# A gated delta-net kernel: state scaling, value masks and small copies made on GpSimd

## The chip, the cores and the metric

The kernel runs on one core of a Trainium2 chip. The time is the device time of one execution in microseconds; a run's figure is the median of its executions, and the chip's profiler records one execution more, with every instruction of every engine. The engines are named as the profile names them: PE (TensorE matmul), PEld (its weight loads), DVE (VectorE), ACT (ScalarE), POOL (GpSimd) and SP (which issues the DMAs). Each engine runs its own queue strictly in order, and engines wait for each other on semaphores.

## The reference, cut to what matters

A two-layer decoder step: an mLSTM layer, then a gated delta-net layer, each followed by an MLP and LayerNorms. 512 prompt tokens and 8 sequences of 4 sample tokens go through together, 544 columns in all. In the delta-net layer the projected rows pass a causal convolution of width 4; the chunked form inverts a triangular matrix for each chunk and head; and every head's state S is decayed and updated.

```python
xp = jnp.concatenate([conv0, qkv], axis=1)            # 3 rows of history, then the new rows
c = xp[:, 0:T] * conv_w[0]
for j in range(1, CONV_W):
    c = c + xp[:, j:j + T] * conv_w[j]
c = jax.nn.silu(c)
new_conv = xp[:, T:]
...
A = M + jnp.eye(L)                                    # M strictly lower triangular
sol = lax.linalg.triangular_solve(A, rhs, left_side=True, lower=True)
...
S = gL_c[..., None, None] * S + jnp.einsum('bhsk,bhsv->bhkv', kdec_c, v_new)
```

## The kernel before

All matrices are held transposed, with features on the 128 partitions and the 544 columns along the free side. A projection (`proj`, L193, through `mm3`, L153) splits each 128x1024 weight tile into two fp32r halves on ACT (L111) and DVE (L112) and issues 48 matmuls of 272 columns on line L158. These are the bulk of PE's work and fill the time between the steps of the delta-net layer.

That layer has eight units of two heads. The list `ORDER` (L58) names its steps, letter and unit: `p` projects and convolves, `a` prepares (`prepare`, with a long chain of small DVE instructions on `xb`, L1085 and L1087, and a DMA round trip that lands as the tile `xc`), `i` inverts (`invert`), `s` scans, `d` decodes the sample tokens of two units, `u` updates their states, `y` and `w` gate and project the output. The steps of `a i s d u` are recorded at a higher priority, and a list scheduler of the language interleaves everything; what comes out is one fixed order for each engine. In what follows i0 to i7 are the eight inversions and u0 to u3 the four updates.

The parts that the change touches:

- `conv`: zeroes three columns of the tile `pre` (L947), copies the old rows into it (L948), lets ACT fill in the new ones, copies 27 columns out through `cvo` (L953, L954), and multiplies by the weights (L958 on ACT, L960 on DVE). Lines L967 and L972 then form the sample part of the result in two instructions.
- `project`: copies one 32-column block of `kqx` to its neighbour (L998).
- `invert`: spreads `xc` over the block-diagonal tile `X` with one masked product of 1024 columns (L1102); PE transposes `X` next (L1117).
- `decode`: for each sample sequence copies 32 columns into one of two buffers `kz` (L1241), the weights of eight small matmuls (L1244).
- `update`: for each half `q` of the eight sequences it makes two value masks `VM` of 512 columns (L1328), in two buffers that both halves share, so the masks of the second half must wait for the matmuls of the first. For each head pair `h0` it loads two state tiles `sst` (`state`, four buffers shared with `decode`), issues six matmuls (L1337) into two PSUM banks, and for each of four sequences of a tile takes state times decay plus product (L1344), then stores the tile (L1345).

The PSUM tag `s`, which those two banks belong to, has two buffers in all (`BANKS`, L37), and `scan` and `decode` use them too.

## Time and profile before

| | |
|---|---|
| median of 3 runs | 1838.17 us (1834.11 to 1847.94) |
| the profiled execution's own time | 1844.15 us |
| its span, first to last instruction | 1842.4 us |
| mean granted PE clock over the span | 0.98 of full speed |
| instructions on POOL | 40, 18.6 us busy |

Sums that come out of the profile are made against 1844.15 us. The delta-net layer lies between about 690 and 1480 us of the span. A granted clock of 1.00 is PE's upper level of 2.4 GHz, and 0.50 its lower one of 1.2 GHz. PE's instructions are pipelined, and the end of a matmul is modelled, so a high busy share of PE does not by itself say that nothing waits.

### The profile page before, as it was taken

The numbers are of one execution on the slowest core, as the hardware profiler recorded it, in microseconds if no ns is written. First come the engines' busy times: TensorE is split into PE (matmuls) and PEld (weight loads), VectorE is DVE, ScalarE is ACT, GpSimd is POOL, SyncE is SP. The second block draws the span as 40 slices with busy tenths as digits, with TensorE's granted clock in tenths as the row PEclk, the third lists the DMA queues.
The fourth block names the chain that finished last, engine by engine and source line by source line (L and its number), as shares of the span: only waits on it lengthen the run. The fifth ranks groups of instructions, "written<-read, shape, count | busy, mean of one in ns | idle before, by whom it ended". The sixth has DMA issues, their size and how long they took to land.

```text
span 1842.4 us, 34187 instructions
## 1 busy us (share of the span) xinstructions
PE 1784.1 (97%) x13868; PEld 1697.9 (92%) x13868; DVE 1070.9 (58%) x2638; ACT 834.8 (45%) x1894; POOL 18.6 (1%) x40
## 2 busy tenths in 40 slices
PE   7999999999999999899999999999999999999997
PEld 7999998999999998897988898899888999999996
DVE  7464767432344377775767757775768643234436
ACT  6454356421233157673657356446436532124314
POOL 2000000000000000000000000000000000000000
PEclk9999999999999998997999999999999999999998
DMA  4122222232233221313232423331332222322311
GB/s 159 58 104 70 70 86 92 81 92 85 88 92 104 85 63 58 102 44 120 58 99 63 127 65 103 100 101 59 88 107 84 81 92 81 92 91 82 113 60 50
DMA packets 84286, 158.78 MB, mean 86 GB/s; under 512 B 37536, under 2 KB 41504, under 8 KB 83616
## 3 DMA queue, kind: packets, MB, share of 16 engines
q1 hardware_dynamic: 84128, 156.60, 28.0%
q8 instruction: 109, 1.79, 0.4%
q14 instruction: 49, 0.40, 0.1%
HBM read 140.51 MB, written 16.06 MB: 85 GB/s over the span
## 4 chain that ended last, share of the span: by engine, by line
PE 82%; DVE 9%; ACT 5%; DMA 3%; issue 1%; SPq 0%; ACTq 0%; DVEq 0%
PE pg_t L158 39%; PE pm_s L158 12%; PE pm_a L158 12%; PE pm_a L1111 4%; PE pm_s L1337 1%; PE pm_s L1181 1%; DVE lnt L342 1%; DVE lnt L343 1%; PE pm_s L1193 1%; PE pm_a L1051 1%; PE pm_s L1201 1%; PE pm_s L1244 1%; DVE acc L960 1%; PE pm_a L1132 1%; PE pm_s L1211 1%
## 5 line engine op out<-in xcount | busy, mean ns | idle before, releaser
L112 DVE TENSOR_TENSOR wl<-wraw,wh 128x1024 fp32r<-128x1024 f32 x200 | 244.7, 1223 | 371.4 <-ACT wh L111 367.6
L158 PE MATMUL pg_t<-XH,wh 128*128 128x272 f32 x1480 | 440.2, 298 | 8.8 <-ACT XH L111 7.2
L158 PE MATMUL pg_t<-XH,wl 128*128 128x272 f32 x1480 | 435.1, 294 | 0.5 <-DVE wl L112 0.5
L158 PE MATMUL pg_t<-XL,wh 128*128 128x272 f32 x1480 | 434.9, 294 | 0.0
L111 ACT CAST wh<-wraw 128x1024 fp32r<-128x1024 f32 (+1 forms) x201 | 210.4, 1047 | 480.7 <-PE pg_t L158 234.6
L158 PEld LDWEIGHTS pg_t<-XH,wh 128*128 128x128 f32 x1480 | 280.6, 190 | 12.5 <-ACT XH L111 7.2
L158 PEld LDWEIGHTS pg_t<-XH,wl 128*128 128x128 f32 x1480 | 280.0, 189 | 2.7 <-issue 1.3
L158 PEld LDWEIGHTS pg_t<-XL,wh 128*128 128x128 f32 x1480 | 280.4, 189 | 2.0 <-issue 1.0
L158 PE MATMUL pg_t<-h,wh 128*128 128x272 f32 x672 | 129.1, 289 | 0.0
L158 PEld LDWEIGHTS pg_t<-h,wh 128*128 128x128 f32 x672 | 105.7, 188 | 0.3
L158 PE MATMUL pg_t<-h,wl 128*128 128x272 f32 x336 | 96.9, 288 | 0.0
L158 PE MATMUL pm_a<-h,wh 128*128 128x272 f32 x496 | 95.3, 288 | 0.0
L158 PE MATMUL pm_s<-h,wh 128*128 128x272 f32 x496 | 94.9, 288 | 0.0
L158 PE MATMUL pm_s<-XH,wh 128*128 128x272 f32 x288 | 84.4, 293 | 0.0
L158 PE MATMUL pm_s<-XH,wl 128*128 128x272 f32 x288 | 83.9, 291 | 0.0
L158 PE MATMUL pm_s<-XL,wh 128*128 128x272 f32 x288 | 83.7, 291 | 0.0
L158 PE MATMUL pm_a<-XL,wh 128*128 128x272 f32 x280 | 81.6, 291 | 1.0 <-DVE XL L354 0.8
L158 PE MATMUL pm_a<-XH,wh 128*128 128x272 f32 x280 | 82.0, 293 | 0.1
L158 PE MATMUL pm_a<-XH,wl 128*128 128x272 f32 x280 | 80.7, 288 | 0.0
L960 DVE SCALAR_TENSOR_TENSOR acc<-pre,cst,acc 128x568 f32<-128x568 f32 x96 | 76.8, 800 | 4.7 <-ACT acc L958 4.3
L158 PEld LDWEIGHTS pm_s<-h,wh 128*128 128x128 f32 x496 | 77.9, 188 | 0.2
L158 PEld LDWEIGHTS pm_a<-h,wh 128*128 128x128 f32 x496 | 78.0, 188 | 0.1
(558 smaller groups left out, 3938.0 us busy)
## 6 DMA issues: line engine op xcount, KB each, us to landing
wraw<-in_w SPq DMA_DIRECT2D x64, 512.0 KB, 3.6
wraw<-in_wb SPq DMA_DIRECT2D x48, 512.0 KB, 3.6
wraw<-in_w2a SPq DMA_DIRECT2D x32, 512.0 KB, 3.6
wraw<-in_wa SPq DMA_DIRECT2D x24, 512.0 KB, 3.6
wraw<-in_w2b SPq DMA_DIRECT2D x24, 512.0 KB, 3.7
sst<-in_s0b SPq DMA_DIRECT2D x32, 256.0 KB, 3.4
sst<-in_s SPq DMA_DIRECT2D x32, 256.0 KB, 3.4
out_ss<-sst SPq DMA_DIRECT2D x32, 256.0 KB, 2.3
```

Of the source, the lines that this page charges most:

```text
L111: S.copy(hi, src)
L112: V.tensor_tensor(lo, src, r32(hi), op=ALU.subtract)
L158: T.matmul(ps, lhsT=wt[:, k, :], rhs=xt[k][:, HS[h]], start=first and k == 0 and q == 0, stop=last and k == n - 1 and q == 2,)
L342: V.tensor_tensor(t, x, rs, op=ALU.mult)
L343: V.tensor_tensor(t, t, mu, op=ALU.subtract)
L960: V.scalar_tensor_tensor(acc, pre[:, q:q + WC], cw[q], acc, op0=ALU.mult, op1=ALU.add)
L1051: T.matmul(pk[:, q * 256:(q + 1) * 256], lhsT=kq[:, 0, c0:c0 + P], rhs=kq[:, :, c0:c0 + P], start=True, stop=True)
L1111: T.matmul(ps[:, c], lhsT=left[:, c], rhs=right[:, c], start=True, stop=True)
L1132: T.transpose(pt[:, c], X[:, c0 + c, 0:m], ident)
L1181: T.matmul(pks[:, w], lhsT=kq[:, w, cc], rhs=St, start=True, stop=True)
L1193: T.matmul(pv[:, j], lhsT=X[:, 4 * (ch // 2) + 2 * j + ch % 2], rhs=rhs[:, j] if ch else vtok[:, j, 0], start=True, stop=True)
L1201: T.matmul(pS, lhsT=ktok[:, ch], rhs=vd, start=True, stop=True)
```

## The change

Six groups of instructions go from DVE to POOL: the zeroing and the copies of `conv`, the copy of `kqx`, the product that makes `X` (one instruction becomes eight, one for each 16-column block), the copies into `kz`, and the masks `VM` (one of 512 columns becomes four of 128). In `update` the state tile is now multiplied by its decay on POOL ahead of time, four instructions of 128 columns for a tile, and what stays on DVE is one addition of 512 columns. The sample part of the convolution's result becomes one instruction in place of two, for which the tile `acc` is three columns wider.

```diff
--- before.py
+++ after.py
@@ -944,16 +944,17 @@
 
 
             pre = cv("pre", W)
-            V.memset(pre[:, 0:3], 0.0)
-            V.tensor_copy(samp(pre)[:, :, 0:3], cvt[:, slot])
+            G.memset(pre[:, 0:3], 0.0)
+            G.tensor_copy(samp(pre)[:, :, 0:3], cvt[:, slot])
             S.copy(pre[:, 3:3 + HN], pss[0])
             S.copy(pre[:, 3 + HN:3 + TP], pss[1][:, :TP - HN])
             S.copy(samp(pre)[:, :, 3:7], pss[1][:, TP - HN:HN].rearrange("p (b t) -> p b t", t=TS))
             cvo = gp.tile([P, 27], F32, tag="cvo", name="cvo", bufs=2)
-            V.tensor_copy(cvo[:, 0:3], pre[:, TP:TP + 3])
-            V.tensor_copy(cvo[:, 3:27].rearrange("p (b t) -> p b t", t=3), samp(pre)[:, :, 4:7])
+            G.tensor_copy(cvo[:, 0:3], pre[:, TP:TP + 3])
+            G.tensor_copy(cvo[:, 3:27].rearrange("p (b t) -> p b t", t=3), samp(pre)[:, :, 4:7])
             dma(o_conv[:, ct, :], cvo)
-            acc = cv("acc", WC)
+            accw = cv("acc", W)
+            acc = accw[:, 0:WC]
             cw = [cst[:, C_CW + 4 * ct + q:C_CW + 4 * ct + q + 1] for q in range(4)]
             S.activation(acc, pre[:, 0:WC], AF.Copy, scale=cw[0])
             for q in range(1, 4):
@@ -963,13 +964,8 @@
             dp = acc[:, 0:TP] if dp is None else dp
             V.tensor_tensor(dp, acc[:, 0:TP], sgm[:, 0:TP], op=ALU.mult)
 
-            a3, s3 = acc[:, TP + 3:WC], sgm[:, TP + 3:WC]
-            V.tensor_tensor(
-                ds[:, 0:7],
-                a3[:, 0:49].rearrange("p (b t) -> p b t", t=7)[:, :, 0:4],
-                s3[:, 0:49].rearrange("p (b t) -> p b t", t=7)[:, :, 0:4],
-                op=ALU.mult)
-            V.tensor_tensor(ds[:, 7], a3[:, 49:53], s3[:, 49:53], op=ALU.mult)
+            a3, s3 = (t[:, TP + 3:W].rearrange("p (b t) -> p b t", t=7)[:, :, 0:4] for t in (accw, pre))
+            V.tensor_tensor(ds, a3, s3, op=ALU.mult)
             return dp, pre[:, 0:TP]
 
         def spare():
@@ -995,7 +991,7 @@
                 pss = first.pop(0) if first else proj(wb[base + w])
                 xs = kqx[:, w, j0].rearrange("p (b t) -> p b t", t=TS)
                 dst, sq = conv(ct + w, cvt, w, kq[:, w], xs, pss)
-                V.tensor_copy(kqx[:, w, j0 + 1], kqx[:, w, j0])
+                G.tensor_copy(kqx[:, w, j0 + 1], kqx[:, w, j0])
                 pt = mtile("t")
                 if w == 0:
                     for ch in range(NCH):
@@ -1099,9 +1095,8 @@
 
             U = st["U"]
             X = tl("X", n=8, bufs=NX)
-            V.tensor_tensor(
-                X.rearrange("p s (b j) -> p s b j", j=16), st["xc"].unsqueeze(2).to_broadcast([P, 8, 8, 16]),
-                bm16.unsqueeze(1).unsqueeze(3).to_broadcast([P, 8, 8, 16]), op=ALU.mult)
+            for b in range(8):
+                G.tensor_scalar(X[:, :, 16 * b:16 * b + 16], st["xc"], bm16[:, b:b + 1], None, op0=ALU.mult)
             def half(t, w, o):
                 return t.rearrange("p c (b x) -> p c b x", x=2 * w)[:, :, :, o:o + w]
 
@@ -1238,7 +1233,7 @@
                 kz.append(z.rearrange("p (r h x) -> p r h x", r=2, h=4))
             for bb in range(NB):
                 st, z = state(s0b[g, :, bb]), kz[bb % 2]
-                V.tensor_copy(z[:, :, :, 28:32], ua["kqx"][:, :, :, TS * bb:TS * bb + TS])
+                G.tensor_copy(z[:, :, :, 28:32], ua["kqx"][:, :, :, TS * bb:TS * bb + TS])
                 for w in range(2):
                     for h in range(4):
                         T.matmul(pkq[32 * h:32 * h + 32, w], lhsT=z[:, w, h, 28 - TS * bb:60 - TS * bb], rhs=st[:, h],
@@ -1325,11 +1320,16 @@
                 VM = []
                 for w in range(2):
                     VM.append(tl("VM", ("tok", "sx")[w], dt=F32R))
-                    V.tensor_tensor(VM[w], vhl[:, w:w + 1].to_broadcast([P, 4, P]),
-                                    bmask[:, 4 * q:4 * q + 4].unsqueeze(2).to_broadcast([P, 4, P]), op=ALU.mult)
+                    for r in range(4):
+                        G.tensor_scalar(VM[w][:, r], vhl[:, w], bmask[:, 4 * q + r:4 * q + r + 1], None, op0=ALU.mult)
                 for h0 in (0, 2):
 
+                    glc = (ua if h0 == 0 else ub)["glc"]
                     sts = [state(s0[g, :, h, 4 * q:4 * q + 4]) for h in (h0, h0 + 1)]
+                    for j in range(2):
+                        for r in range(4):
+                            bb = NCH + 4 * q + r
+                            G.tensor_scalar(sts[j][:, r], sts[j][:, r], glc[:, j, bb:bb + 1], None, op0=ALU.mult)
                     pS = [mtile("s").rearrange("p (b d) -> p b d", b=4) for _ in range(2)]
                     for i, (a, b) in enumerate(((0, 0), (0, 1), (1, 0))):
                         for j in range(2):
@@ -1337,11 +1337,7 @@
                             T.matmul(pS[j], lhsT=khr[o:o + 32, a], rhs=VM[b][o:o + 32], start=(i == 0), stop=(i == 2),
                                      tile_position=(o, 0))
                     for j in range(2):
-                        glc = (ua if h0 == 0 else ub)["glc"][:, j]
-                        for r in range(4):
-                            bb = 4 * q + r
-                            t = sts[j][:, r]
-                            V.scalar_tensor_tensor(t, t, glc[:, NCH + bb:NCH + bb + 1], pS[j][:, r], op0=ALU.mult, op1=ALU.add)
+                        V.tensor_tensor(sts[j], sts[j], pS[j], op=ALU.add)
                         dma(o_ss[g, :, h0 + j, 4 * q:4 * q + 4], sts[j])
 
         def gate_out(g, oTs, osm):
```

The scheduler lays out a new order from this. Three places of it matter for the prediction. The first is PE in u1, between the last matmuls (L1337) on the masks of the first half and the first ones on those of the second, before; the rows left out are 27, of them 21 projections (L158):

```order
L1337 MATMUL pm_s<-VM,khl 128x512 x3
L158 MATMUL pg_t<-gyh,wh 128x272
...
L158 MATMUL pg_t<-gyl,wh 128x272
L158 MATMUL pg_t<-gyh,wl 128x272
L1337 MATMUL pm_s<-VM,khl 128x512 x6
L1027 MATMUL pm_t<-ident,acc 128x128 x4
L1337 MATMUL pm_s<-VM,khl 128x512 x6
```

The same place after, line L1337 as before:

```order
L1056 MATMUL pm_a<-RRb,hmr 128x256 x2
L1337 MATMUL pm_s<-VM,khl 128x512 x3
L158 MATMUL pg_t<-gyh,wh 128x272
L158 MATMUL pg_t<-gyl,wh 128x272
L158 MATMUL pg_t<-gyh,wl 128x272
L158 MATMUL pg_t<-gyh,wh 128x272
L158 MATMUL pg_t<-gyl,wh 128x272
L158 MATMUL pg_t<-gyh,wl 128x272
L1337 MATMUL pm_s<-VM,khl 128x512 x6
L158 MATMUL pg_t<-gyh,wh 128x272
```

Between the two halves there stood 30 rows of PE's queue; now there are six projections.

The second place is the making of those masks for the second half of u1. Before, it stands on DVE, where U and A are products of `prepare`:

```order
L1344 SCALAR_TENSOR_TENSOR sst<-sst,glc,pm_s 128x128
L1069 TENSOR_TENSOR A<-pm_a,Eh 128x256
L1344 SCALAR_TENSOR_TENSOR sst<-sst,glc,pm_s 128x128
L1328 TENSOR_TENSOR VM<-vhl,bmask 128x512 x2
L1068 TENSOR_TENSOR U<-pm_a,Eh 128x256
L1069 TENSOR_TENSOR A<-pm_a,Eh 128x256
```

After, it stands on POOL, where X is the inversion's tile (L1099), VM the masks (L1324) and sst the scaled states (L1332):

```order
L947 MEMSET pre 128x3
L948 COPY pre<-cvt 128x8x3
L1099 TENSOR_SCALAR X<-xc,bm_150 128x8x16 x8
L953 COPY cvo<-pre 128x3
L954 COPY cvo<-pre 128x24
L1324 TENSOR_SCALAR VM<-vhl,bmask 128x128 x8
L1332 TENSOR_SCALAR sst<-sst,glc 128x128 x16
L1232 MEMSET kz 128x480 x2
L1099 TENSOR_SCALAR X<-xc,bm_150 128x8x16 x8
```

Two instructions of DVE have become eight of POOL, behind copies of the convolution and ahead of 16 state scalings.

The third is PE around the first transposes of `X` in i0, where `sx` belongs to the decode step; before:

```order
L1282 MATMUL pm_s<-ident,sx 128x128
L158 MATMUL pg_t<-XH_75,wh 128x272
L158 MATMUL pg_t<-XL_83,wh 128x272
L158 MATMUL pg_t<-XH_75,wl 128x272
L158 MATMUL pg_t<-XH_76,wh 128x272
L158 MATMUL pg_t<-XL_84,wh 128x272
L158 MATMUL pg_t<-XH_76,wl 128x272
L158 MATMUL pg_t<-XH_77,wh 128x272
L158 MATMUL pg_t<-XL_85,wh 128x272
L1117 MATMUL pm_a<-ident,X 128x128 x8
L1287 MATMUL pm_s<-sx 128x128
```

And after, with the transposes on L1112:

```order
L1277 MATMUL pm_s<-ident,sx 128x128
L158 MATMUL pg_t<-XL_90,wh 128x272
L158 MATMUL pg_t<-XH_82,wl 128x272
L158 MATMUL pg_t<-XH_75,wh 128x272
L158 MATMUL pg_t<-XL_83,wh 128x272
L158 MATMUL pg_t<-XH_75,wl 128x272
L158 MATMUL pg_t<-XH_76,wh 128x272
L158 MATMUL pg_t<-XL_84,wh 128x272
L158 MATMUL pg_t<-XH_76,wl 128x272
L1112 MATMUL pm_a<-ident,X 128x128 x8
L1282 MATMUL pm_s<-sx 128x128
```

The transposes still stand behind eight projections; the work ahead of them that makes `X` has moved to POOL.

## Rows read from the trace of the kernel before

**Rows 1.** The page's head and part 1: busy time of each engine.

```profile
span 1842.4 us, 34187 instructions
...
PE 1784.1 (97%) x13868; PEld 1697.9 (92%) x13868; DVE 1070.9 (58%) x2638; ACT 834.8 (45%) x1894; POOL 18.6 (1%) x40
```

**Rows 2.** The page's part 4: the chain that ended last, by engine.

```profile
PE 82%; DVE 9%; ACT 5%; DMA 3%; issue 1%; SPq 0%; ACTq 0%; DVEq 0%
```

**Rows 3.** Busy time by stretch: PE, PEld, DVE, ACT, POOL, granted PE clock, DMA share.

```profile
400.00:500.00 100.00, 100.00 (x800) 100.00 (x799) 28.22 (x34) 20.30 (x23) 0.00 (x0) 1.00 0.29 89
690.00:1480.00 790.00, 764.61 (x5941) 698.27 (x5939) 562.35 (x1638) 443.46 (x1129) 4.71 (x9) 0.96 0.30 86
754.30:757.80 3.50, 0.29 (x3) 0.07 (x1) 3.50 (x11) 2.56 (x4) 0.00 (x0) 0.99 0.01 2
757.80:761.20 3.40, 3.10 (x14) 2.94 (x14) 3.40 (x19) 3.37 (x12) 0.00 (x0) 0.50 0.11 18
832.40:839.60 7.20, 4.35 (x25) 2.92 (x23) 6.67 (x21) 1.05 (x1) 0.00 (x0) 1.00 0.61 166
839.60:863.50 23.90, 23.90 (x108) 19.27 (x107) 10.60 (x31) 7.73 (x18) 0.93 (x2) 0.50 0.42 132
```

**Rows 4.** PE's waits, 690 to 1480 us: total us, times, longest us.

```profile
PE pm_t L1002 <- DVE xb L1087: 3.5, 1, 3.5
PE pm_s L1337 <- DVE VM L1328: 2.3, 1, 2.3
...
PE pm_s L1337 <- DVE sst L1344: 1.4, 2, 0.8
```

**Rows 5.** Groups of POOL's instructions, by shape: busy us, mean ns, idle before.

```profile
L280 POOL TENSOR_SCALAR_AFFINE_SELECT bd<-bd 128x128 f32<-128x128 f32 x2 | 2.2, 1104 | 0.0
...
L279 POOL TENSOR_SCALAR_AFFINE_SELECT bd<-o 128x128 f32<-128x128 f32 x2 | 1.2, 622 | 0.0
...
L244 POOL TENSOR_SCALAR_AFFINE_SELECT b<-b 128x128 f32<-128x128 f32 x1 | 0.5, 538 | 0.0
L243 POOL TENSOR_SCALAR_AFFINE_SELECT b<-z 128x128 f32<-128x128 f32 x1 | 0.5, 517 | 0.0
...
L237 POOL TENSOR_SCALAR_AFFINE_SELECT f<-z 128x128 f32<-128x128 f32 x1 | 0.3, 292 | 0.0
L252 POOL TENSOR_SCALAR_AFFINE_SELECT rowm<-o 128x32 f32<-128x32 f32 x1 | 0.2, 217 | 0.0
```

**Rows 6.** Groups of DVE's instructions, by shape, columns as above.

```profile
L1344 DVE SCALAR_TENSOR_TENSOR sst<-sst,glc,pm_s 128x128 f32<-128x128 f32 x128 | 36.3, 342 | 21.9 <-PE pm_s L1337 21.0 <-DMA sst<-in_s 0.6
...
L964 DVE TENSOR_TENSOR acc<-acc,pre 128x512 f32<-128x512 f32 x16 | 10.9, 683 | 2.2 <-ACT pre L475 2.0
...
L1328 DVE TENSOR_TENSOR VM<-vhl,bmask 128x512 fp32r<-128x512 f32 x16 | 10.5, 682 | 0.0
...
L1102 DVE TENSOR_TENSOR X<-xc,bm 128x1024 f32<-128x1024 f32 x8 | 9.7, 1218 | 0.3 <-DMA xc<-dx 0.3
...
L948 DVE COPY pre<-cvt 128x24 f32<-128x24 f32 x32 | 5.8, 183 | 0.0
...
L947 DVE MEMSET pre<- 128x3 f32 x32 | 2.0, 61 | 0.1
```

**Rows 7.** Timelines of DVE and PE at i0, i4 and i6: start us, duration us.

```profile
774.62 1.23 DVE L1102 TENSOR_TENSOR X<-xc,bm 128x1024 f32<-128x1024 f32 x1 [0.28 <-DMA xc<-dx]
...
775.90 1.09 PE L1117 MATMUL pm_a<-ident,X 128*128 128x128 f32 x8
...
1048.49 1.22 DVE L1102 TENSOR_TENSOR X<-xc,bm 128x1024 f32<-128x1024 f32 x1
...
1058.51 1.04 PE L1117 MATMUL pm_a<-ident,X 128*128 128x128 f32 x8
...
1234.90 1.22 DVE L1102 TENSOR_TENSOR X<-xc,bm 128x1024 f32<-128x1024 f32 x1
...
1240.77 0.71 PE L1117 MATMUL pm_a<-ident,X 128*128 128x128 f32 x5
```

## The prediction

> **What bounds the kernel now.** I read the page's head first: PE is busy 97% of the span, DVE 58%, POOL 1% [rows 1]; then the chain that ended last, 82% of it PE [rows 2]. So time taken off DVE counts only where PE stands waiting for DVE, and time added to POOL counts only where PE ends up waiting for POOL. Next the stretches [rows 3]. In 400:500 PE issues 800 projections in 100 us, 0.125 us each, which is as dense as it gets and my price for one projection as cover. In 690:1480, the delta-net layer, PE is idle for 790 - 764.6 = 25.4 us, and the granted clock averages 0.96, so some 0.04 x 790 = 32 us of clock are lost. These two, 57 us, are all that the layer can give back, whatever DVE is spared.
>
> How the clock is lost shows in the same group: PE is busy for 0.29 of 3.5 us (754.3:757.8) and the next 3.4 us run at 0.50, the 1.2 GHz level; it is busy for 4.35 of 7.2 us (832.4:839.6, inside u0) and the next 23.9 us run at 0.50, filled with the small matmuls of i1 and u0. An idle gap of 2.3 to 3.5 us [rows 4] is thus paid a second time: 3.4 us at half speed lose at least 1.7 us, and the long stretch up to 12.
>
> **What one POOL instruction costs.** The trace of before has no multiplication on POOL. Its nearest rows are nine affine selects of 128x128 f32, which read SBUF and write SBUF: two of 1104 ns, two of 622, one of 538, one of 517, one of 292 and two more rows that repeat it [rows 5]; mean 0.60 us. A mask, a state scaling and a block of X each cover 128 columns too. I take 0.60 and keep 0.29 and 1.10 as ends. The small copies (24 to 32 columns) I take at the 0.2 us of the 32-column select [rows 5], against 0.18 on DVE [rows 6]. In total: 256 instructions x 0.60 + 144 copies x 0.2 = 182 us of POOL over some 600 us, so POOL does not become a bound by its sum; it counts where a burst of eight stands in front of PE.
>
> The Trainium skill (GPSIMD Engine Reference, section 4.1, Engine selection) calls one-input work on GpSimd roughly line-rate, which would put these instructions at the lower end, 0.29 us, and the time near that of rival (c) below. The selects are one-input work as well, and six of the nine took 517 ns or more, so the rows speak for more than that.
>
> **Part 1: the masks.** Eight instructions of 0.60 us, 4.8 us, replace two of DVE of 0.68. The second half's masks share their buffers with the first's, so POOL can begin only when the last matmul of the first half has read them, and PE cannot go on before the last is written. What stands between the two on PE is therefore the whole cover, in the new order ten projections in u0 (1.25 us), six in u1 (0.75), six in u3 (0.75), and in u2 six small matmuls and a transpose, 0.13 us each by the eight transposes in 1.04 us [rows 7], so 0.9. PE waits 4 x 4.8 - 3.65 = 15.6 us; 2.3 of that is there already [rows 4]. **+13 us** (at 0.29: +3; at 1.10: +29). In u1 the cover shrank from 30 rows of the queue to six.
>
> **Part 2: X.** Eight instructions, 4.8 us, replace one of 1.2 [rows 6]: +3.6 us between the landing of `xc` and the transposes. In i0 the transposes start 0.05 us after X is done [rows 7]; this stands for five of the eight inversions (0.05 to 0.33 us). i5 has 1.1 us to spare, i4 8.8 and i6 4.6 [rows 7]. Five at 3.5 and one at 2.5 make 20. Two places move: i1's transposes now stand behind 44 more projections (5.5 us), which covers it, -3.5; i6's lose 47 projections (5.9 us) and with them their spare time, +4. **+20 us** (at 0.29: +5; at 1.10: +45).
>
> **Part 3: scaled states.** PE never reads them; it waits only through the two banks of tag `s`, which the addition on DVE must empty. Both pairs of the first half are scaled long before. In the second half a pair of tiles is scaled by 4.8 us after the masks and added by 5.5. Against PE's order this fits in u1 and u2, and is late by about 1 us in u0, where the X of i1 stands between the two tiles, and by 0.8 in u3. **+2 us** (0 to +17). What queues behind a late addition: on DVE the weight splits L112, on SP the store L1341 and behind it the next weight load.
>
> **Part 4: small work.** The copies into `kz` have two buffers and come one by one between matmuls, as before: +1 (0 to +5). In the convolution the zeroing and the copy of old rows now stand behind bursts of 16 to 32 POOL instructions, 10 to 19 us; ACT's L958 waits for them, and behind it on ACT the emptying of the projection banks. Mostly a tile is prepared well ahead, so with SP's share from part 3 I take +4 (0 to +10). The copies to `cvo` are hidden: only a store waits for them. The wider `acc` and the merged product cost nothing that PE sees.
>
> **Part 5: the clock.** Six new gaps of 2.5 to 4 us (X; the updates u1 to u3 have their half-speed stretches already) at 1.7 us: **+10** (0 to +17). Against it, the new order puts projections among the matmuls of i1 and u0, and the 23.9 us at half speed should mostly go: **-8** (0 to -12).
>
> **Part 6: DVE's relief.** State: 36.3 - 32 x 0.68 = 14.4 us; masks 10.5; X 9.7 [rows 6]; six small groups, from the 5.8 of L948 down to the 2.0 of L947 [rows 6], 26 together; the merged pair 5. That is 66 us off DVE's 562 in this layer [rows 3]. PE sees of it what it waited for DVE here: the 1.4 us for the state updates [rows 4] and a part of the 3.5 us for `xb` and the shorter waits like it: **-6** (0 to -12).
>
> **The sum.** 13 + 20 + 2 + 1 + 4 + 10 - 8 - 6 = +36 us. Against the profiled execution's 1844.15 that is 1880; that execution lies 6 us above the median of the runs, so I predict **1874 us**, 2% slower.
>
> **The rivals.** (a) POOL and DVE get in each other's way. DVE is busy 71% of the layer [rows 3], mostly with instructions of 0.2 to 1.2 us [rows 6]; if a POOL instruction often has to let one of these finish, 0.25 us on top of 0.60 is a fair mean. At 0.85 us the masks cost +21, X +32, states and queues +13, the clock +10, the gains shrink to -9: +67, **1905 us**. In the trace of before POOL is idle beside DVE, apart from the setup, so nothing speaks for or against it. The Trainium skill states this rule (SBUF — State Buffer, Who interferes with whom): a DVE instruction with two SBUF inputs contends with a GpSimd instruction that reads SBUF, and the later one waits for the whole of the other. No row here shows it. It speaks against this change, since the additions, the splits L112 and the convolution L960 are of that kind.
>
> (b) PE's gaps are mostly waits that would have come anyway. While PE stands for POOL, DVE and ACT catch up, and half of the 25 idle us of before vanish (-13), and the clock does not fall for the X gaps (-10): +13, **1851 us**. For it: the idle time is in many short waits. Against: the gaps of before each stand at one line for one producer [rows 4].
>
> (c) Faster. The place is u0 with i1: the half-speed stretch after 839.6 goes entirely (-12), the relief is whole (-12), and POOL's price is at the lower end, so that masks and X cost only +3 and +5, the rest +2: -14, **1824 us**. It turns on one number, POOL's instruction: at 0.35 us masks and X cost about 12 and the sum crosses zero; below that the kernel is faster. One of the groups in [rows 5] is below it, three of its nine instructions.
>
> **How the numbers follow.** Forecast 0.42, (a) 0.17, (b) 0.25, (c) 0.16. A measurement of this kernel can tell about 1%, 18 us, from no change. Slower by more than that are the forecast and (a): 0.59. (c) is split, since 1824 is within 1%: faster by over 1% 0.11, and within 1% 0.30. The range leaves out the far half of (a), and half of (c): 1822 to 1912. With the price at its upper end everywhere the sum would be far above, about +120; I leave that out, since only two of the nine selects were that long.
>
> **What would show it.** In the profile after, POOL's groups for VM, X and sst at 0.5 to 0.7 us each (below 0.35: (c); above 0.8: (a)); PE waiting for POOL at the matmuls of `update` for 3 to 5 us in each of four places, and at the transposes of X for 2.5 to 4 us in five or six; no wait of PE for VM on DVE; the granted clock above 0.9 where u0 and i1 lie, but short half-speed stretches behind the gaps at X; DVE at about 1005 us busy (more means that it is held up by POOL). The forecast is wrong if PE's waits for POOL add up to under 15 us, or if the stretches at half speed shrink by more than the gaps add.

## The result, and the profile after

The changed kernel takes 1926.69 us (median of 4 runs, 1923.26 to 1929.63) against 1841.22 for the kernel before: ratio 1.0464, 95% interval 1.0417 to 1.0511. It is 85.5 us slower where 36 were forecast, and above the upper end of the range, 1912.

The page of the changed kernel, head, part 1 and part 4 [rows 1, 2]:

```profile
span 1927.9 us, 34433 instructions
...
PE 1816.9 (94%) x13868; PEld 1722.6 (89%) x13868; DVE 1033.6 (54%) x2310; ACT 832.3 (43%) x1894; POOL 244.6 (13%) x472
...
PE 28%; DVE 4%; POOL 2%; DMA 2%; ACT 1%; issue 1%; SPq 0%; POOLq 0%; ACTq 0%; DVEq 0%
```

DVE is busy 37 us less, POOL 226 us more, and PE, which runs the same 13868 instructions, is busy 33 us *more*. Most of that is the clock's, as the next rows show. They give the layer and its half-speed stretches by window (columns as in [rows 3]): first the layer of the kernel before, two of its seven stretches and the sum of all seven; then the layer of the changed kernel, five of its 17 stretches and the sum of all 17:

```profile
690.00:1479.90 789.90, 764.51 (x5940) 698.17 (x5939) 562.25 (x1638) 443.39 (x1128) 4.71 (x9) 0.96 0.30 86
...
1181.01:1187.83 6.82, 6.82 (x32) 4.42 (x31) 4.32 (x14) 2.02 (x4) 0.00 (x0) 0.50 0.56 174
...
1355.09:1361.91 6.82, 6.82 (x25) 5.46 (x27) 4.50 (x13) 0.00 (x0) 0.00 (x0) 0.50 0.59 185
sum 61.44, PE 59.32 PEld 49.24 DVE 34.72 ACT 19.58 POOL 1.86; mean PE 8.47 PEld 7.03 DVE 4.96 ACT 2.80 POOL 0.27
```

```profile
690.00:1565.40 875.40, 797.90 (x5959) 723.37 (x5958) 526.28 (x1316) 441.23 (x1131) 231.90 (x441) 0.93 0.27 78
...
781.08:787.90 6.82, 3.15 (x15) 3.15 (x16) 0.00 (x0) 1.34 (x3) 3.62 (x7) 0.50 0.01 2
839.10:852.75 13.65, 10.82 (x36) 7.92 (x35) 5.90 (x14) 2.16 (x4) 9.58 (x15) 0.50 0.68 191
863.00:873.24 10.24, 10.24 (x49) 9.38 (x49) 5.14 (x10) 0.97 (x4) 3.65 (x7) 0.50 0.67 206
927.85:941.50 13.65, 13.20 (x63) 13.16 (x64) 2.59 (x5) 4.63 (x7) 0.61 (x2) 0.50 0.00 0
...
1006.36:1016.60 10.24, 5.73 (x24) 5.37 (x24) 0.94 (x3) 4.07 (x12) 4.46 (x8) 0.50 0.00 0
...
sum 129.70, PE 108.26 PEld 95.59 DVE 42.45 ACT 37.59 POOL 54.81; mean PE 6.37 PEld 5.62 DVE 2.50 ACT 2.21 POOL 3.22
```

The layer, taken from 690 us to 362.5 us before the end in both kernels, grew by 85.5 us, all that the span grew by. (An estimated 2.8 us of it arose ahead of 690 us: by then the changed kernel has 5159 matmuls behind it and the kernel before 5181, and 22 projections at 0.125 us [rows 3] make 2.8.) Three parts make it up. PE idle: 875.4 - 797.9 = 77.5 against 25.4, +52.1. Clock: PE is busy 108.3 us at 0.50, the 1.2 GHz level, against 59.3 in the seven stretches of before (61.4 us long); half of such time is counted as lost, +24.5. A rest of 9 us is neither.

Whom PE waits for between 690 and 1570 us (total, times, longest) [rows 4]:

```profile
PE pm_a L1112 <- POOL X L1099: 31.4, 7, 7.0
PE pm_s L1337 <- POOL VM L1324: 12.5, 4, 3.6
PE pg_t L303 <- DVE XR L358: 5.9, 2, 4.3
...
PE pm_a L1047 <- DVE kqx L968: 3.9, 1, 3.9
...
PE pm_s L1239 <- POOL kz L1236: 2.5, 3, 1.0
...
PE pm_s L1337 <- DVE sst L1340: 1.5, 1, 1.5
```

POOL is waited for 46.4 us. Its groups (busy, mean ns, idle before), and then the same three lines with shortest, median and longest duration:

```profile
L1332 POOL TENSOR_SCALAR sst<-sst,glc 128x128 f32<-128x128 f32 x128 | 87.0, 698 | 22.6 <-DMA sst<-in_s 9.8 <-issue 7.4 <-DMA dg<-U 3.1
L1324 POOL TENSOR_SCALAR VM<-vhl,bmask 128x128 fp32r<-128x128 f32 x64 | 49.2, 787 | 75.0 <-PE pm_s L1337 57.6 <-DVE tb L1081 12.2 <-DVE xb L1083 3.0
L1099 POOL TENSOR_SCALAR X<-xc,bm 128x128 f32<-128x128 f32 x64 | 42.2, 676 | 62.5 <-DMA xc<-dx 62.5
L948 POOL COPY pre<-cvt 128x24 f32<-128x24 f32 x32 | 14.3, 448 | 0.0
```

```profile
L1332 POOL TENSOR_SCALAR sst<-sst,glc x128: 595/602/1607, 772.0 to 1453.5; 128x128 f32<-128x128 f32 x128
L1324 POOL TENSOR_SCALAR VM<-vhl,bmask x64: 597/602/2700, 802.3 to 1442.0; 128x128 fp32r<-128x128 f32 x64
L1099 POOL TENSOR_SCALAR X<-xc,bm x64: 595/598/1481, 779.4 to 1406.4; 128x128 f32<-128x128 f32 x64
```

The timelines of POOL, then of PE, at i0 show one such wait with all that it brings [rows 7]:

```profile
771.99 5.94 POOL L1332 TENSOR_SCALAR sst<-sst,glc 128x128 f32<-128x128 f32 x8 [1.40 <-DMA sst<-in_s]
777.88 0.72 POOL L953 COPY cvo<-pre 128x3 f32<-128x3 f32 x1
...
779.44 5.25 POOL L1099 TENSOR_SCALAR X<-xc,bm 128x128 f32<-128x128 f32 x8
...
784.75 1.97 PE L1112 MATMUL pm_a<-ident,X 128*128 128x128 f32 x8 [6.97 <-POOL X L1099]
```

POOL works without a pause from 772.0: eight scalings of states, four small instructions of `conv`, then X. PE runs dry at 777.8, its clock falls at 781.08 while it waits, and the transposes that it waited for take 1.97 us; on DVE's X they took 1.09 [rows 7].

### The profile page after: what moved, and what is told of

It reads as the page before. It is cut to its first block, busy times and chain, and to the rows that moved or that the text cites. A ratio compares the mean times of both kernels' runs of the same rounds, so it can differ in the third digit from the quotient of the medians.

```text
span 1927.9 us, 34433 instructions
## 1 busy us (share of the span) xinstructions
PE 1816.9 (94%) x13868; PEld 1722.6 (89%) x13868; DVE 1033.6 (54%) x2310; ACT 832.3 (43%) x1894; POOL 244.6 (13%) x472
## 5 line engine op out<-in xcount | busy, mean ns | idle before, releaser
L158 PE MATMUL pg_t<-XH,wh 128*128 128x272 f32 x1480 | 444.3, 300 | 8.1 <-ACT XH L111 7.0
L112 DVE TENSOR_TENSOR wl<-wraw,wh 128x1024 fp32r<-128x1024 f32 x200 | 245.5, 1227 | 377.7 <-ACT wh L111 376.3
L158 PE MATMUL pg_t<-XH,wl 128*128 128x272 f32 x1480 | 439.9, 297 | 0.5 <-DVE wl L112 0.5
L158 PE MATMUL pg_t<-XL,wh 128*128 128x272 f32 x1480 | 440.0, 297 | 0.0
L158 PEld LDWEIGHTS pg_t<-XH,wh 128*128 128x128 f32 x1480 | 284.5, 192 | 13.4 <-ACT XH L111 7.0
L158 PEld LDWEIGHTS pg_t<-XL,wh 128*128 128x128 f32 x1480 | 284.3, 192 | 3.1 <-issue 1.9
L158 PEld LDWEIGHTS pg_t<-XH,wl 128*128 128x128 f32 x1480 | 283.8, 192 | 3.4 <-issue 1.9
L158 PE MATMUL pg_t<-h,wh 128*128 128x272 f32 x672 | 129.2, 289 | 0.0
L158 PEld LDWEIGHTS pg_t<-h,wh 128*128 128x128 f32 x672 | 105.8, 189 | 0.3
L158 PE MATMUL pg_t<-h,wl 128*128 128x272 f32 x336 | 97.0, 289 | 0.0
L158 PE MATMUL pm_a<-h,wh 128*128 128x272 f32 x496 | 95.4, 289 | 0.0
L158 PE MATMUL pm_s<-h,wh 128*128 128x272 f32 x496 | 95.0, 288 | 0.0
L1332 POOL TENSOR_SCALAR sst<-sst,glc 128x128 f32<-128x128 f32 x128 | 87.0, 698 | 22.6 <-DMA sst<-in_s 9.8
L358 DVE SCALAR_TENSOR_TENSOR XR<-XR,pg_t 128x272 f32<-128x272 f32 x118 | 50.9, 433 | 64.7 <-PE pg_t L158 64.4
L158 PE MATMUL pm_s<-XH,wh 128*128 128x272 f32 x288 | 84.2, 292 | 0.0
L158 PE MATMUL pm_s<-XH,wl 128*128 128x272 f32 x288 | 83.9, 291 | 0.0
L158 PE MATMUL pm_s<-XL,wh 128*128 128x272 f32 x288 | 83.6, 290 | 0.0
L158 PE MATMUL pm_a<-XL,wh 128*128 128x272 f32 x280 | 82.0, 293 | 1.0 <-DVE XL L354 0.8
L158 PE MATMUL pm_a<-XH,wh 128*128 128x272 f32 x280 | 82.4, 294 | 0.0
L158 PE MATMUL pm_a<-XH,wl 128*128 128x272 f32 x280 | 81.1, 290 | 0.0
```

Of the source, the lines that this page charges most:

```text
L112: V.tensor_tensor(lo, src, r32(hi), op=ALU.subtract)
L158: T.matmul(ps, lhsT=wt[:, k, :], rhs=xt[k][:, HS[h]], start=first and k == 0 and q == 0, stop=last and k == n - 1 and q == 2,)
L358: V.scalar_tensor_tensor(x, x, ALPHA if first else 1.0, ps, op0=ALU.mult, op1=ALU.add)
L1332: G.tensor_scalar(sts[j][:, r], sts[j][:, r], glc[:, j, bb:bb + 1], None, op0=ALU.mult)
```

## The experiments

All were timed against the kernel before. The table splits each layer as above: idle time of PE, half-speed time (in brackets PE's busy part of it), and the rest, which is the layer less the idle time less half of the bracket. The ratios go by medians, the other columns by the one profiled execution, which lies up to 6 us beside its kernel's median (e5's 4.8 under it, e7's 4.4 above); differences of a few us between rows are within that.

| run | ratio, 95% interval | layer us | PE idle | half speed | rest |
|---|---|---|---|---|---|
| before | 1 | 789.9 | 25.4 | 61.4 (59.3) | 734.8 |
| after | 1.0464 (1.0417 to 1.0511) | 875.4 | 77.5 | 129.7 (108.3) | 743.8 |
| e1 X on DVE | 1.0191 (1.0150 to 1.0233) | 816.8 | 48.6 | 51.2 (44.3) | 746.0 |
| e2 masks on DVE | 1.0390 (1.0354 to 1.0426) | 857.0 | 71.1 | 105.8 (87.5) | 742.2 |
| e3 both on DVE | 1.0141 (1.0106 to 1.0176) | 813.2 | 39.9 | 58.0 (53.2) | 746.7 |
| e4 early fill | 1.0486 (1.0443 to 1.0529) | 882.4 | 70.2 | 88.8 (73.0) | 775.7 |
| e4b fill at X | 1.0434 (1.0407 to 1.0461) | 868.5 | 53.0 | 75.1 (61.9) | 784.6 |
| e5 scaling only | 1.0086 (1.0064 to 1.0109) | 795.6 | 32.3 | 40.9 (40.0) | 743.3 |
| e6 small work only | 1.0086 (1.0067 to 1.0106) | 799.2 | 28.8 | 51.2 (48.6) | 746.2 |
| e7 merged product only | 1.0052 (1.0031 to 1.0072) | 798.7 | 29.2 | 51.2 (46.0) | 746.5 |
| e8 X in one product | 1.0288 (1.0247 to 1.0329) | 840.6 | 57.9 | 85.3 (70.4) | 747.5 |
| e9 X split | 1.0315 (1.0275 to 1.0356) | 845.9 | 59.7 | 102.4 (86.4) | 743.0 |
| e10 before, filled | 0.9978 (0.9956 to 1.0001) | 786.1 | 23.6 | 44.4 (39.5) | 742.8 |
| e11 all as products | 1.0121 (1.0082 to 1.0161) | 810.3 | 39.8 | 47.8 (46.0) | 747.5 |

**e1, e2, e3: undoing the two steps that PE waits for.** The edits, in `invert` and in `update`:

```diff
-            for b in range(8):
-                G.tensor_scalar(X[:, :, 16 * b:16 * b + 16], st["xc"], bm16[:, b:b + 1], None, op0=ALU.mult)
+            V.tensor_tensor(X.rearrange("p s (b j) -> p s b j", j=16), st["xc"].unsqueeze(2)...,
+                bm16.unsqueeze(1)..., op=ALU.mult)                      # e1, e3
-                    for r in range(4):
-                        G.tensor_scalar(VM[w][:, r], vhl[:, w], bmask[:, 4 * q + r:4 * q + r + 1], ...)
+                    V.tensor_tensor(VM[w], vhl[:, w:w + 1]..., bmask[:, 4 * q:4 * q + 4]..., op=ALU.mult)   # e2, e3
```

> The changed kernel with one edit undone: the operand X of the inversion's transposes is made on VectorE again, in one product of 1024 columns; masks, state scaling and small copies stay on GpSimd. Theory A (TensorE takes its work in order and stands idle until the eighth GpSimd product of a burst is done, and then pays a second time, because its clock falls to half speed around those gaps): the 31 us of TensorE's waits at the transposes go back to a few us and about half of the 33 us lost to the clock come back, so about 1880 us, ratio 1.02 (1870 to 1890). Theory B (VectorE and GpSimd slow each other; the price is collisions): 64 of 472 GpSimd instructions are gone, so about 15 us less, 1912, ratio 1.04. Theory C (the order of the work that the changed scheduler costs give is itself the worse one, whatever GpSimd's price): 1915 to 1935.

> The changed kernel with one edit undone: the value masks are made on VectorE again, one product of 512 columns for each two of the state update; X, state scaling and small copies stay on GpSimd. Theory A (waits in order, then the clock): TensorE's 12.5 us of waits for the masks go, X no longer queues behind mask bursts of 8 us, and some 5 to 8 us of half-speed loss come back: about 1905 us, ratio 1.035 (1895 to 1912). Theory B (collisions of VectorE and GpSimd): about 1915 to 1920. Theory C (the order): 1915 to 1935.

> The changed kernel with X and the value masks both made on VectorE again; the states are still scaled on GpSimd, the update is one addition, the small copies are on GpSimd. Theory A (waits in order, then the clock): all waits of TensorE for bursts are gone, the half-speed stretches are back near the 61 us of the kernel before: about 1855 us, ratio 1.008 (1842 to 1868). Theory B (collisions): 128 scalings and 176 small instructions of GpSimd, well over half of its time, remain and still collide with VectorE: 1885 or more. Theory C (the order): 1915 to 1935.

PE's wait for X in e1, then in e2:

```profile
PE pm_a L1113 <- DVE X L1098: 2.8, 2, 2.3
```

```profile
PE pm_a L1112 <- POOL X L1099: 32.1, 7, 7.0
```

Measured 1875.6, 1912.2 and 1866.4 us. X alone gives back 51 us, as theory A had it; collisions alone (theory B) would have left 1912 and the order alone (theory C) 1915 to 1935. It pays through idle time (77.5 to 48.6) and through the clock (108.3 to 44.3 us at half speed, 32 us). The masks give back 14 us where about 21 were expected, which is just past theory A's range: with X left on POOL, PE still waits 32.1 us for it. What theory A missed is that e3 stays 1.4% above the kernel before.

Every edit also lets the scheduler lay out a new order, so e1 by itself does not exclude that a part of the 51 us is the order's: compared row by row, about 1400 of PE's 13868 matmuls stand elsewhere in e1 than in the changed kernel. For e8 and e11 below it is at most 165 and 263, so what these two win back is hardly the order's.

**e4, e4b: filling the wait.** Both add work and leave the rest of the changed kernel alone. In e4:

```diff
+                for k in range(28 if c0 == 0 else 0):
+                    T.matmul(pt[:, :HN], lhsT=onesr, rhs=XH[k % KD][:, HS[0]], start=True, stop=True)
                 for c in range(4):
                     T.transpose(pt[:, c], X[:, c0 + c], ident)
```

> The changed kernel with work added: ahead of the first transposes of X in each of the 8 inversions TensorE runs 28 matmuls of 272 columns on data that is long there, into the bank that the transposes then overwrite. They are some 28 x 0.12 = 3.4 us of TensorE work at full speed, 28 us in all, and stand where it waited 31 us for X. Theory A's second half (half speed comes from the idle gaps): the wait for X falls from 31 to about 8 us, half-speed stretches in the layer fall from about 129 us to about 90, and the kernel is 10 to 20 us faster for 28 us of added work: about 1910. If the half-speed stretches don't come from these gaps: their sum stays near 129 us and the time is between 1927 and 1955.

The added matmuls depended on nothing late, so in six of the eight inversions they ran 11 to 35 us ahead of the transposes. They filled little of it (20.8 us for X remain), and took 37.6 us of PE. The half-speed time fell to 88.8 us all the same, but the time did not fall, 1930.6 us; what brought the clock up can't be told here. e4b reads the very data that X is made from:

```diff
+                for k in range(24 if c0 == 0 else 0):
+                    T.matmul(pt[:, 0], lhsT=ident, rhs=st["xc"].rearrange("p s j -> p (s j)"), start=True, stop=True)
```

> The filling of TensorE's wait for X once more: the added matmuls now read the data that X is made from, so that they can't run ahead of the wait: 24 of 128 columns ahead of the first transposes in each inversion, into the bank that the transposes overwrite, an estimated 24 x 0.11 = 2.6 us in each (by the 109 ns between TensorE's transposes of the same shape), 21 us of added work in all. Theory A's second half (half speed comes from the idle gaps at X): the wait for X falls from 31 to 12 us or less, half-speed stretches in the layer from 129 to 90 us or less, time 1900 to 1920. If the half-speed stretches don't come from these gaps: their sum stays at 115 us or more, and the time is 1925 to 1945.

PE's waits and the added line's busy time in the layer, for e4b:

```profile
PE pm_s L1339 <- POOL VM L1326: 13.4, 4, 4.0
...
PE pm_a L1114 <- POOL X L1099: 3.1, 1, 3.1
```

```profile
690.00:1558.50 868.50, 49.45 (x384) 47.34 (x384) 0.96 0.27 78
```

Each added matmul is recorded twice (384 for 192), and PE got 49 us of extra work and not 21; yet the kernel is no slower for it: 1920.3 us. The wait for X is 3.1 us, the half-speed time 75.1. Two things pay for the added work: 24.5 us of idle time filled, and 46.4 fewer busy us at half speed, 23.2 us. The 3.1 us that remain are all in i0, and there a stretch of 10.24 us at half speed remains too; the stretches behind X in i2, i3, i5, i6 and i7 are gone. The gaps at X thus cost about as much again in clock as in waiting.

**e5, e6, e7: what is left with X and masks on DVE.** e7 is the kernel before with the merged product and the wider `acc`; e5 adds the scaling of states on POOL to it, e6 the small copies and memsets.

```diff
-            a3, s3 = acc[:, TP + 3:WC], sgm[:, TP + 3:WC]
...
-            V.tensor_tensor(ds[:, 7], a3[:, 49:53], s3[:, 49:53], op=ALU.mult)
+            a3, s3 = (t[:, TP + 3:W].rearrange("p (b t) -> p b t", t=7)[:, :, 0:4] for t in (accw, pre))
+            V.tensor_tensor(ds, a3, s3, op=ALU.mult)        # all three
...
+                            G.tensor_scalar(sts[j][:, r], sts[j][:, r], glc[:, j, bb:bb + 1], None, op0=ALU.mult)
...
+                        V.tensor_tensor(sts[j], sts[j], pS[j], op=ALU.add)      # e5
...
+            G.tensor_copy(samp(pre)[:, :, 0:3], cvt[:, slot])                  # e6, and its like
```

> Of the change only the state update: states scaled on GpSimd ahead of it and one addition of 512 columns on VectorE; X, masks and all small copies on VectorE as before (the product that the change merged stays merged). X and masks undone together left 1.4% over the kernel before; this asks what that rest is. Theory D (VectorE's additions wait for GpSimd's scalings: 22 us of such waits with X and masks undone, and TensorE behind them): most of the rest is still here, ratio 1.010 (1.006 to 1.014), about 1857 us. Theory E (the small copies, at 0.28 to 0.5 us on GpSimd, sit in chains that TensorE waits for): ratio 1.002 (0.998 to 1.005).

> Of the change only the small work: the small convolution copies, the copies of kqx and kz and their memsets on GpSimd; X, masks and the state update on VectorE as before, four scale-and-add steps of 128 columns. Theory D (the rest lies with the scaled states): ratio 1.003 (0.998 to 1.006), about 1843 us. Theory E (it lies with the small copies): ratio 1.010 (1.006 to 1.014), about 1857 us.

> Of the change only what neither GpSimd nor the update needs: the merged product ahead of the convolution; everything on VectorE as in the kernel before. Theories D and E both: as the kernel before, ratio 1.000 (0.997 to 1.003). A third one, F (the rest is a matter of the order that this product shifts): ratio 1.008 or more.

D and E each miss one of the two runs, and both miss e7: the rest is spread. The merged product alone costs 0.5%, and either step on top of it 0.3 to 0.4% more, with intervals of e5 and e6 that just overlap e7's. In e7 the table shows where: idle +3.8, clock -6.7, rest +11.7 us. One wait can be named. The first line is of e7 and is the same in every run that has the merged product (L968); the second is its counterpart in the kernel before:

```profile
PE pm_a L1047 <- DVE kqx L968: 3.9, 1, 3.9
```

```profile
PE pm_a L1051 <- DVE kq L964: 2.1, 1, 2.1
```

Every run with the merged product has a rest of 742 to 748 us where nothing was added, against 734.8; e10, which is without it, has 742.8 less its 5.8 us of added work, 737.0. PE has the same instructions; they are spaced more widely at full clock, in e7 by 7.5 us counted group by group, of which the projections from XH and XL have 3.5 and the matmuls on `kz` 2.3, and the remainder is small at many lines. Theory F, that the order around the new instruction does it, stays open: about 1300 of PE's matmuls stand elsewhere in e7 than before, but F's own figure, 1.008 or more, was not reached, and no run changes the order alone.

**e8, e9: the price of X on POOL.** e8 makes X on POOL in the one product that DVE used; e9 makes half of X on DVE.

```diff
-            for b in range(8):
-                G.tensor_scalar(X[:, :, 16 * b:16 * b + 16], st["xc"], bm16[:, b:b + 1], None, op0=ALU.mult)
+            G.tensor_tensor(X.rearrange("p s (b j) -> p s b j", j=16), st["xc"]..., bm16..., op=ALU.mult)   # e8
+            V.tensor_tensor(X[:, :, 0:64].rearrange("p s (b j) -> p s b j", j=16), ..., op=ALU.mult)        # e9
+            for b in range(4, 8):
+                G.tensor_scalar(X[:, :, 16 * b:16 * b + 16], st["xc"], bm16[:, b:b + 1], None, op0=ALU.mult)
```

> The changed kernel with X made on GpSimd by one product of two operands over 1024 columns in place of eight scalings of 128. Theory G (GpSimd's price lies with the instruction): one instruction takes under 2.5 us, TensorE's wait for X falls from 31 to under 12 us, the time to about 1890 us. Theory H (it lies with the columns: the line through 0.2 us for 24 columns and 0.6 us for 128, both undisturbed in the trace of the changed kernel, gives an estimate of 4.1 us for 1024, and a second operand may add to that): 4 to 8 us, the waits for X stay at 25 us or more, time 1920 to 1960.

> The changed kernel with four of the eight blocks of X made on VectorE, in one product of 512 columns, and four on GpSimd: the burst on GpSimd is half as long, about 2.4 us. Theory A, waits and half speed both in the measure of a gap's length: the wait for X falls from 31 to about 10 us, half-speed stretches from 129 to about 85 us, time 1885 to 1900. If any gap at X brings the clock down, however short: waits about 10 us, half-speed stretches 110 us or more, time 1900 to 1912.

POOL's group of e8 and PE's wait for it, then the same of e9:

```profile
L1098 POOL TENSOR_TENSOR X<-xc,bm 128x1024 f32<-128x1024 f32 x8 | 16.9, 2113 | 64.4 <-DMA xc<-dx 64.3
...
PE pm_a L1113 <- POOL X L1098: 10.8, 5, 3.9
```

```profile
L1102 POOL TENSOR_SCALAR X<-xc,bm 128x128 f32<-128x128 f32 x32 | 26.6, 845 | 76.4 <-DMA xc<-dx 76.4
...
PE pm_a L1115 <- POOL X L1102: 12.6, 5, 4.5
```

One product of 1024 columns takes 2.1 us where eight scalings took 4.65 at best: theory G's price. The wait for X falls to 10.8 us, the time to 1896.2. e9's four scalings take 845 ns each, 3.4 us and not 2.4; its wait is 12.6 us. Its time (1900.5) lies on the border of its two cases and its half-speed time (102.4) between them: a shorter gap costs less. Whether it does so in proportion stays open: e8, with a wait of 10.8 us, has 85.3 us at half speed.

**e10: the mechanism in the kernel before.** Six matmuls of 512 columns at the one gap of [rows 3] that stood ahead of 23.9 us at half speed:

```diff
+                    for k in range(6 if (g, q, h0) == (0, 1, 0) else 0):
+                        T.matmul(pS[0], lhsT=ident, rhs=done[0], start=True, stop=True)
+                    done = sts
```

> The kernel before with work added at one place: six matmuls of 512 columns on finished states in the first state update, ahead of its second half, where TensorE waited 2.3 us for a mask and then ran 23.9 us at half speed. An estimate of 6 x 0.43 = 2.6 us of TensorE work. Theory A's second half (the gap brought the clock down): the stretch of 23.9 us is gone or under 8 us, some 8 to 10 us come back, ratio 0.995 (0.992 to 0.998), faster than both kernels. If that stretch has another cause: it stays and the time is 0 to 3 us more, ratio 1.000 to 1.002.

The timeline of PE at this place, and the half-speed stretches of e10 on either side of it:

```profile
834.01 1.59 PE L1340 MATMUL pm_s<-VM,khl 32*128 32x512 f32 x6
836.24 3.67 PE L1335 MATMUL pm_s<-sst,ident 128*128 128x512 f32 x8 [0.64 <-PE pm_s L1340]
839.74 1.04 PE L1117 MATMUL pm_a<-ident,X 128*128 128x128 f32 x8
```

```profile
757.00:760.41 3.41, 2.93 (x13) 2.77 (x14) 3.41 (x17) 3.38 (x12) 0.00 (x0) 0.50 0.06 5
1009.58:1019.82 10.24, 8.32 (x27) 6.71 (x28) 7.81 (x26) 4.26 (x11) 0.00 (x1) 0.50 0.67 213
```

The stretch is gone. The half-speed time of the layer falls by 17 us and not by 23.9, since two later stretches are 3.4 us longer each. Eight of the twelve records of the added matmuls fill the gap; the other four came later, among the matmuls of i1, from 840.6 us on, where the stretch had begun at 839.67 before, so filling the gap and adding work behind it are not quite apart here. PE did 5.8 us of useless work (2.6 were expected; each matmul is recorded twice) and the kernel is not slower, 0.9978 (0.9956 to 1.0001). It is the fastest version tried, though this interval does not tell it from the kernel before.

**e11: all three steps as products.** On e8, each mask and each state scaling in one product of 512 columns:

```diff
+                    G.tensor_tensor(VM[w], vhl[:, w:w + 1]..., bmask[:, 4 * q:4 * q + 4]..., op=ALU.mult)
...
+                        G.tensor_tensor(sts[j], sts[j], glc[:, j, NCH + 4 * q:NCH + 4 * q + 4]..., op=ALU.mult)
```

> The changed kernel with all three of its GpSimd steps in the form that was 1.9 us for X's 1024 columns: X in one product of 1024 columns, each mask in one of 512 in place of four scalings of 128, and the four scalings of a state in one product of 512. Theory G2 (the price lies with the form, two operands at 1.9 ns a column): a mask or state takes 0.95 to 1.2 us in place of 2.4 or more, GpSimd is busy for about 140 us and not 245, TensorE's waits for masks fall from 12.5 to 5 us or less, ratio 1.013 to 1.022, about 1872 us. Theory H2 (what remains hangs on the engine chosen and its queue, not on the price): 1.025 to 1.030, as with X alone in one product. A ratio under 1.005 would say that the change was sound but for the form of its instructions.

POOL's groups, and PE's waits for POOL, of e11:

```profile
L1331 POOL TENSOR_TENSOR sst<-sst,glc 128x512 f32<-128x512 f32 x32 | 37.1, 1173 | 34.7 <-DMA sst<-in_s 23.2 <-PE pm_s L1286 4.2 <-issue 3.6
L1324 POOL TENSOR_TENSOR VM<-vhl,bmask 128x512 fp32r<-128x512 f32 x16 | 19.7, 1254 | 74.4 <-PE pm_s L1337 54.9 <-DVE tb L1081 17.4 <-DVE vhl L1304 2.1
L1098 POOL TENSOR_TENSOR X<-xc,bm 128x1024 f32<-128x1024 f32 x8 | 16.4, 2050 | 70.6 <-DMA xc<-dx 68.9 <-ACT acc L959 1.7
```

```profile
PE pm_a L1113 <- POOL X L1098: 5.2, 4, 1.8
...
PE pm_s L1337 <- POOL VM L1324: 2.2, 2, 1.2
```

1863.7 us, a ratio of 1.0121, just under G2's range: with the same split of work and nearly the same order on PE, the form of POOL's instructions gives back 63 of the 85 us. Theory H2 falls. The 1.2% that stay are about what e5, e6 and e7 show together. What POOL loses beside DVE (below; mean less median duration, over the three groups) is 29 us in the changed kernel, 28 in e8 and 8 in e11: the 31 us that e8 gives back are the form's price, while in the other 32 price and collisions are not told apart.

## Why the prediction was wrong

The direction held, and so did the way to it: PE takes its work in order, POOL's bursts of eight stand in front of it. The sum was +36 us and the layer grew by 85.5. In the prediction's own terms, with what the trace shows in their place:

| term | forecast | measured | by which |
|---|---|---|---|
| part 1, masks | +13 | +10 | PE's waits, 12.5 less 2.3 |
| part 2, X | +20 | +31 | PE's waits, 31.4 less 0.5 |
| parts 3 and 4, states, small work | +7 | +3 | PE's waits for states and `kz` |
| part 5, clock | +10 - 8 | +24.5 | PE's busy time at half speed |
| part 6, relief, with the merged product | -6 | +17 | other idle time +8, rest +9 |

Two steps failed, each by some 23 us: the price of a gap in clock, and the relief. X's queue adds 11.

- **Price of a POOL instruction, 0.60 us.** Right in the median (598 to 602 ns), and that was luck: it is the mean of nine affine selects between 292 and 1104 ns, another operation. The means are 676 to 787 ns. For the small copies 0.2 us was right in the median as well (0.207 for L948) and too low in the mean (0.45).
- **Part 1, masks, +13.** Near: 12.5 us in four places in place of 2.3, so +10.
- **Part 2, X, +20.** The mechanism held: i4 waits for nothing, i1 for 1.2 us, the other six for 3.5 to 7.0. The size didn't: 31.4 us. It priced X's own burst and not POOL's queue ahead of it. In i0 eight scalings and four small instructions end 1.7 us after PE has run dry; in i3 X stands behind an 8.4 us burst of masks. In both, X starts 3.0 us after `xc` has landed, which is 6 of the 11 us; in i2, i5 and i6 the burst itself takes 5.6 to 5.8 us against 4.65 in i3, i4 and i7.
- **Part 3, +2, and part 4, +5.** PE's wait for the states is 1.5 us (1.4 before), for `kz` 2.5. e5 and e6 lie 0.3 to 0.4%, 6 to 7 us, above e7 each, which is of the right order; the table has PE's own waits alone.
- **Part 5, the clock, +10 and -8: the first step that failed.** Measured +24.5. A gap was priced at the shortest stretch, 3.4 us, 1.7 lost, although the seven stretches of before last 8.8 us on average; the 17 of after last 7.6. And the 23.9 us at u0 and i1 should have gone; they are there, as 13.65 and 10.24 us. The prediction had in hand that one gap of 2.3 us was followed by 23.9 us at half speed, and did not price a new gap by it. All six waits for X of 3.5 us or more have a stretch, 3.4 to 13.7 us long, that begins during the wait; in e1 none of the seven stretches that are left has a wait for X ahead of it, and in e4b only the one in i0. So at X the gap brings the clock down: take it away, by a faster engine or by useless work, and the stretch goes. Elsewhere this does not hold for each stretch: the one at 839.10 begins 3.5 us ahead of the wait for the masks, and those of before at 1181.01 and 1355.09 have no idle time of PE of 0.3 us or more in the 9 us ahead of them.
- **Part 6, DVE's relief, -6, and a merged product that "cost nothing that PE sees": the second step that failed.** No relief came. PE's idle time outside POOL's waits grew by 8 us (52.1 less 46.4, and the 2.3 for masks on DVE that went), and the rest by 9. e7 has the merged product alone, is 0.5% slower and has a rest of +11.7, so this rest comes without any work on POOL. The merged product was put at nothing without a row of PE. DVE is busy for 1033.6 us and not for 1005, which the prediction took as a sign that POOL holds it up; but its two largest groups take as long as before (L112 1227 against 1223 ns, the convolution 806 against 800), and its instructions' durations add up to 72 us less. They overlap less, so that its busy time falls by only 37.

Of the rivals, (a) was nearest in time, but not for its reason. POOL's instructions do stretch beside DVE: worked out from this trace, of the 256 masks, scalings and blocks of X the 102 with no DVE instruction beside them average 599 ns, the 49 beside DVE instructions that have one input or read one from PSUM 611 ns, and the 105 beside a DVE instruction with two inputs in SBUF 875 ns. That adds 29 us to POOL's time. The Trainium skill (SBUF — State Buffer, Who interferes with whom) has this rule, and the trace agrees with it on POOL's side. It is a correlation, since no run here took DVE's work away alone. The additions on DVE, which the prediction counted among the kind that contends, read one input from PSUM (`sst<-sst,pm_s`) and are not of it. Rival (a)'s 0.85 us per instruction was not reached, and e8 and e11, which change the form and leave DVE's work, win back 31 and 63 us. (c) turned on one number: below 0.35 us per 128 columns the kernel would be faster. e11 has 1041 ns for 512 columns (median), 0.26 for 128, 0.31 with its collisions, and is 1.2% slower. So that point was wrong too: in e11's layer PE still waits 9.5 us for X, masks and `kz` on POOL, its idle time is 14.4 us above the kernel before, and the rest is 12.7 us above it.

Open: why the merged product costs 0.5%, beyond the 1.8 us of one wait; what brings the clock down where no gap stands ahead; and how the 29 us of stretching divide between PE's path and idle POOL time.

## What to carry to other kernels

Work moved to a slower engine is priced by what stands ahead of it in that engine's queue as well, and each wait that it puts in front of TensorE is to be counted twice, once as idle time and once as clock, with the longest stretch of the trace as the upper end and not the shortest as the middle. Here the clock took half as much as the idle time over the whole layer (24.5 against 52.1 us), and about as much at X alone (e1: 32 against 29; e4b: 23 against 24.5). An instruction that is merged or moved at no cost is still to be tried alone: e7 was slower by 0.5%. Before small pieces go to GpSimd, write them as one product over all columns and not as a scaling per block. Where a gap can't be closed, useless matmuls on data that arrive with the wait cost nothing here (e4b); on data that are long there they ran too early (e4).

## What the runs showed of the hardware

GpSimd scales 128 columns by a value per partition in 0.60 us, but multiplies 512 columns by a broadcast operand in 1.04 and 1024 in 1.92 us (shortest): by the last two, 0.16 us and 1.7 ns a column, so that 128 columns would take an estimated 0.38 us. The Trainium skill (GPSIMD Engine Reference, section 4.1, Engine selection) has one-input work at roughly line-rate and two-input work at half of VectorE's. The second half agrees roughly (1.92 us against 1.22 [rows 6] for X, 1.6 times). The first agrees with a copy of 24 columns (0.207 us in the median against 0.18 [rows 6]), but not for the scaling, which takes 0.60 us against 0.34 for DVE's scale-and-add of the same 128 columns [rows 6]: the one-input form was the slow one here, and the measurement decides.

Beside DVE instructions with two inputs in SBUF, GpSimd's 0.60 us became 0.875 on average; beside DVE's other instructions 0.61.

TensorE was given 49 us more work in e4b and the kernel took no longer; in e10, 5.8 us more did away with a stretch of 23.9 us at half speed.
